# Depthwise convolution of a two-layer encoder: five of eight channel tiles move from VectorE taps to TensorE, and all eight use 32x32 array tiles

## The chip, the cores and the metric

The kernel runs on one core of a Trainium2 chip. The metric is the device time of one execution in microseconds (us). Before the change it is 1244.36 us, the median of three runs (1243.08 to 1247.17). Lower is better.

The core has four compute engines with instruction queues of their own: TensorE (PE in the profile, its weight loads PEld), VectorE (DVE), ScalarE (ACT) and GpSimd (POOL). SyncE (SP) only issues transfers here, and GpSimd issues some too. Matmul results go to PSUM banks, which VectorE and ScalarE read; everything else lies in SBUF, on 128 partitions, or in memory.

## What is computed

One step of a two-layer encoder over 1152 tokens: 1024 of a new stream (the prompt) and 16 of each of 8 running streams (the samples). Layer 0 is attention beside a gated mixing branch. The change lies in layer 1, the convolution layer:

```python
xn = _rmsnorm(x, norm_g)
z = jnp.einsum('btd,de->bte', xn, w_in)              # 1024 -> 3 x 1024
a, b, g = jnp.split(z, [C_WIDTH, 2 * C_WIDTH], axis=-1)
u = a * jax.nn.sigmoid(b)
# 30 earlier rows of u stand ahead: zeros for the prompt, conv_state for each sample
ctx = jnp.concatenate([conv_state, u], axis=1)
c = lax.conv_general_dilated(ctx, w_dw[:, None, :], window_strides=(1,), padding='VALID',
                             feature_group_count=C_WIDTH) + b_dw     # 31 taps per channel
c = jax.nn.silu(_layernorm(c, ln_g, ln_b)) * jax.nn.silu(g)
y = x + jnp.einsum('btc,cd->btd', c, w_out)
return y, ctx[:, -(CONV_WIDTH - 1):]
```

All arithmetic is to the accuracy of float32. A final RMS norm follows.

## The kernel before

**The order.** The program is written in Python; a scheduler places each instruction on its engine's queue by a simulated timeline, so the order on an engine isn't that of the source alone. `issue_after(m)` keeps what is inside it behind the instruction m; `high_priority` moves what is inside forward by an offset. Buffers come from pools with a fixed count (`bufs`); who asks for a buffer waits until its last reader is done.

**Products.** A float32 product is made of three (`mm3`): both operands are split into a high and a low part, and hi·hi, hi·lo and lo·hi are summed in a PSUM bank. A product over 1024 inputs is 24 matmuls ("mm" in the profile). `split_w` fetches weights as raw (SP, three buffers), casts them to wh on ScalarE (L143) and takes wl = raw − wh on VectorE (L144); the pool has four buffers of each. Plain float32 matmuls go through PE in two passes, and the profile has two records for each.

**The convolution layer** (`phase_conv`, `conv_tile`) handles 8 tiles of 128 channels, channels on partitions. For each tile there are three chunks of 384 tokens, and for each chunk two mm3 products of 24: first for b, whose sigmoid ScalarE writes to sb (L1103), then for a, which VectorE multiplies by sb into u. Three PSUM banks hold these products in turn. After each of a tile's six products stands a hook position (0 to 5), at which work of the tile before is put in: at position 1 (`TAIL`) the transposes and copies that write out the last rows of u (un), at the positions in `TOEP` the Toeplitz steps.

Five tiles (0, 1, 3, 5, 7) do the convolution on VectorE (`taps`): 31 instructions over 1024 prompt tokens and 31 over the samples' 8x16. The three tiles of `PE_TILES` (2, 4, 6) do it on TensorE. VectorE writes u to U with time split in 8 phases, U[channel, phase, m]; U is stored to memory (s_u) and read back as X, in which a partition is a pair of channel and phase, 16 channels and 8 phases on 128 partitions, 8 such groups. For a group, five products of 128x128 by 176 columns (py), each with X shifted by one column, make the 31 taps. Their weights tw are block-diagonal, 16 blocks of 8x8, and GpSimd builds them (L1166) from a table wx of shifted taps and the mask `same`. Two groups are a step, at each of four hook positions. ScalarE copies py to Y (L1173); Y goes to memory (s_c, L1176) and comes back as yb with channels on partitions; ScalarE adds the bias into cT (L1180 for the prompt, L1183 twice for the samples). GpSimd sums the cT of tiles 0 to 6 into msum (L952).

Then follow the 8 gate tiles, in pairs that share one load of weights: for each the three mm3 products of the third part of w_in1, and Silu on ScalarE into sg (L1021). After the gate tiles in `LN_AT` stands `norm_chunk`: the layer norm of one 384-token chunk, in which PE sums over channels (ln), ScalarE squares, GpSimd adds squares, and VectorE subtracts the mean and multiplies. At the end VectorE multiplies cT by sg, and the output projection with w_out1 runs over 9 token tiles.

**Setup** (`setup_conv`), long before this layer, transposes the taps and writes tables to memory: s_cc (bias and norm factors, and all taps for VectorE) and s_w (eight shifted copies of the flipped taps of the three tiles).

Of the kernel before, what the change touches and what calls it, by code (L numbers as in the profile page):

```python
# [11 lines left out]
F32 = mybir.dt.float32  # L12
# [10 lines left out]
NB = 8  # L23
# [21 lines left out]
def shape_constants():  # L45
# [26 lines left out]
    same = np.zeros((P, P), np.float32)  # L72
    for p in range(P):
        same[p, p // 8 * 8:p // 8 * 8 + 8] = 1.0
# [7 lines left out]
C_W = C_SAME + P  # L82
PE_TILES = (2, 4, 6)
# [10 lines left out]
TOEP = (2, 3, 4, 5)  # L94
TAIL = 1
LN_AT = (4, 5, 6)
# [6 lines left out]
class Builder:  # L103
# [222 lines left out]
    def setup_conv(self):  # L326
        nc, a = self.nc, self.a
        npe = len(PE_TILES)
        self.s_w = self.dram.tile([npe * P, 8, 40], F32, name="s_w")
        self.s_cc = self.dram.tile([P, 8 * (4 + CONV)], F32, name="s_cc")  # L330
# [9 lines left out]
        nc.gpsimd.dma_start(out=flip, in_=a["cst"][:CONV, C_FLIP:C_FLIP + CONV])  # L340
        ps = self.ptr.tile([P, 512], F32, name="tr")
        for i in range(8):
            nc.tensor.transpose(ps[:, i * CONV:(i + 1) * CONV], wn[:, i * P:(i + 1) * P], self.ident[:CONV, :CONV])
        nc.scalar.copy(cc[:, 32:32 + 8 * CONV], ps[:, :8 * CONV])
        nc.gpsimd.dma_start(out=self.s_cc, in_=cc[:, :32 + 8 * CONV])
        wr = cc[:, 640:640 + npe * 48].rearrange("p (n k) -> p n k", k=48)
        ps = self.ptr.tile([P, 512], F32, name="tr")
        for n, i in enumerate(PE_TILES):
            nc.tensor.matmul(ps[:, n * CONV:(n + 1) * CONV], lhsT=wn[:, i * P:(i + 1) * P], rhs=flip,
                             start=True, stop=True)  # L350
        nc.scalar.copy(wr[:, :, 7:7 + CONV], ps[:, :npe * CONV].rearrange("p (i k) -> p i k", k=CONV))
# [562 lines left out]
    def phase_conv(self):  # L914
        nc, tc, a = self.nc, self.tc, self.a
        with ExitStack() as st:
# [5 lines left out]
            self.pacc = pl.enter_context(tc.tile_pool(name="pac", bufs=1, space=PSUM, reuse_waits="tile"))  # L922
            self.py = self.pacc.tile([P, 512], F32, name="py")
# [5 lines left out]
            cT = [cp.tile([P, TOK], F32, name=f"cT{i}") for i in range(8)]  # L929
            msum = cp.tile([P, TOK], F32, name="msum")  # L930
            cc = cp.tile([P, 8 * (4 + CONV)], F32, name="cc")
            same = cp.tile([P, P], F32, name="same")
            nc.sync.dma_start(out=cc, in_=self.s_cc)
            nc.sync.dma_start(out=same, in_=a["cst"][:, C_SAME:C_SAME + P])
            chan = cc[:, :32].rearrange("p (i n) -> p i n", n=4)
            wdw = cc[:, 32:].rearrange("p (i k) -> p i k", k=CONV)
            npe = len(PE_TILES)
            s_u = self.dram.tile([npe, P * 8, 180], F32, name="s_u")
            s_c = self.dram.tile([npe, P * 8, 176], F32, name="s_c")
            s3 = E(ExitStack())  # L940
            u_p = s3.enter_context(tc.tile_pool(name="up", bufs=2, side="right", reuse_waits="tile"))
            with tc.tile_pool(name="ub", bufs=2, reuse_waits="tile") as ub:
                prev = None
                self.last_tap = None

                def finish(i, f):
                    if f is not None:
                        f()
                    if i == 1:
                        nc.gpsimd.tensor_tensor(msum, cT[0], cT[1], ALU.add)  # L950
                    elif 1 < i < 7:
                        nc.gpsimd.tensor_tensor(msum, msum, cT[i], ALU.add)  # L952

                for i in range(8):
# [3 lines left out]
                    if prev is not None:  # L958
                        hooks[TAIL] = [prev[0]]
                        for p, f in zip(TOEP, prev[1]):  # L960
                            hooks.setdefault(p, []).append(f)
# [100 lines left out]
    def conv_tile(self, i, wb, pm, u_p, ub, cv, chan, wdw, scr, same, hooks):  # L1062
# [100 lines left out]
        def step(q):  # L1163
# [10 lines left out]
            if q < 3:  # L1174
                return
# [37 lines left out]
```

## Time and profile before

| | |
|---|---|
| median of three runs | 1244.36 us (1243.08 to 1247.17) |
| the profiled execution's own time | 1244.07 us |
| its span in the profile | 1242.3 us |
| mean granted TensorE clock | 0.975 of full speed |
| PE busy | 1163.6 us, 94% |
| DVE busy | 807.9 us, 65% |
| ACT busy | 461.0 us, 37% |
| POOL busy | 364.3 us, 29% |

The profile is of one execution. The span runs from the first to the last recorded instruction, and the time of the execution has 1.8 us around it. A row of a group of instructions names the line in the kernel, the engine, the operation, what is written and read (out<-in by the program's names), shapes, the count, the busy time and the mean of one; behind the bar at its end, the engine's idle time ahead of it and who ended it. A wait row reads: engine, waiting tile and line, the releaser, total us, times, longest. The convolution layer and the gate tiles lie between about 776 and 1160 us of the span.

### The profile page before, as it was taken

To read this page: it belongs to the slowest core of one execution; us is meant where nothing else is said; L and a number is where in the kernel's file an instruction comes from. 1 tells how busy PE (TensorE), PEld (TensorE's weight loads), DVE (VectorE), ACT (ScalarE), POOL (GpSimd) and SP (SyncE) were. 2 spreads that over 40 slices of the span, in tenths; PEclk is the share of its full clock that TensorE was granted. 3 is DMA by queue.
4 is the path that set the end of the run, shared out by engine and by line. 5 is a ranking of instruction groups with operands and counts; after the bars stand their busy time and mean duration, and the time that the engine had idled before them with its cause. 6 is when DMAs were issued, how large, how long until landed. Compare 5 with 4: busy or idle time off the path is not lost.

```text
span 1242.3 us, 18215 instructions
## 1 busy us (share of the span) xinstructions
PE 1163.6 (94%) x6516; PEld 1038.4 (84%) x6516; DVE 807.9 (65%) x1663; ACT 461.0 (37%) x1058; POOL 364.3 (29%) x516
## 2 busy tenths in 40 slices
PE   6999999999989997779999998999999987998997
PEld 4878998999989987557776767999999987997886
DVE  5420225688787778765555444899989999267843
ACT  4431223545454545554435334111121212256421
POOL 2232223344354335322322220112424220033300
PEclk9999999999989998889999999999999998999999
DMA  8352444414141314877766646113321310212231
GB/s 298 107 157 73 148 145 136 126 55 120 41 122 46 103 49 137 287 246 238 238 220 237 194 145 174 45 41 89 97 85 60 112 60 24 68 35 102 80 124 68
DMA packets 122042, 153.23 MB, mean 123 GB/s; under 512 B 13697, under 2 KB 85401, under 8 KB 121944
## 3 DMA queue, kind: packets, MB, share of 16 engines
q1 hardware_dynamic: 107968, 108.21, 28.1%
q0 software_dynamic: 13840, 43.60, 10.5%
q8 instruction: 52, 0.85, 0.3%
q14 instruction: 38, 0.31, 0.1%
q10 hardware_dynamic: 144, 0.26, 0.1%
HBM read 116.22 MB, written 36.26 MB: 123 GB/s over the span
## 4 chain that ended last, share of the span: by engine, by line
PE 75%; DMA 9%; DVE 6%; issue 5%; ACT 3%; POOL 1%; SPq 0%; DVEq 0%; POOLq 0%; ACTq 0%
PE mm L155 51%; PE out L155 7%; PE py L1172 3%; PE pa L587 2%; PE tr L416 2%; DMA vraw<-in_cache_v 1%; PE tr L165 1%; PE S L544 1%; PE mm L784 1%; PE S L545 1%; PE mm L783 1%; PE tr L582 1%; DMA big<-s_c 1%; DMA s_c<-big 1%; PE S L730 1%
## 5 line engine op out<-in xcount | busy, mean ns | idle before, releaser
L155 PE MATMUL mm<-yh,wh 128*128 128x384 f32 x576 | 196.4, 341 | 15.2 <-ACT sg L1021 12.7
L155 PE MATMUL mm<-yh,wl 128*128 128x384 f32 x576 | 195.4, 340 | 0.2 <-DVE wl L144 0.2
L155 PE MATMUL mm<-yl,wh 128*128 128x384 f32 x576 | 195.4, 339 | 0.0
L155 PE MATMUL mm<-wh,xh 128*128 128x384 f32 (+1 forms) x504 | 185.4, 369 | 1.5 <-DVE sg L467 0.6
L1148 DVE SCALAR_TENSOR_TENSOR acc<-u,cc,acc 128x1024 f32<-128x1024 f32 x145 | 185.7, 1281 | 0.4
L155 PE MATMUL mm<-wl,xh 128*128 128x384 f32 (+1 forms) x504 | 184.3, 366 | 1.5 <-DVE wl L144 1.5
L155 PE MATMUL mm<-wh,xl 128*128 128x384 f32 (+1 forms) x504 | 183.5, 364 | 0.0
L144 DVE TENSOR_TENSOR wl<-raw,wh 128x1024 fp32r<-128x1024 f32 (+1 forms) x72 | 91.3, 1275 | 91.8 <-ACT wh L143 88.4
L155 PEld LDWEIGHTS mm<-yh,wh 128*128 128x128 f32 x576 | 109.2, 190 | 16.0 <-ACT sg L1021 13.0
L155 PEld LDWEIGHTS mm<-yh,wl 128*128 128x128 f32 x576 | 109.1, 190 | 0.6 <-DVE wl L144 0.5
L155 PEld LDWEIGHTS mm<-yl,wh 128*128 128x128 f32 x576 | 109.2, 190 | 0.3
L155 PEld LDWEIGHTS mm<-wh,xh 128*128 128x128 f32 x504 | 95.7, 190 | 13.1 <-issue 1.1
L155 PEld LDWEIGHTS mm<-wl,xh 128*128 128x128 f32 x504 | 95.6, 190 | 11.4 <-DVE wl L144 2.9
L155 PEld LDWEIGHTS mm<-wh,xl 128*128 128x128 f32 x504 | 95.5, 189 | 8.8 <-DVE xl L168 0.3
L143 ACT CAST wh<-raw 128x1024 fp32r<-128x1024 f32 (+1 forms) x72 | 71.4, 1001 | 70.0 <-PE mm L155 32.2
L124 POOL TENSOR_TENSOR rr<-pw,mhalf 128x1 f32<-128x1 f32 x59 | 38.4, 651 | 165.9 <-DVE pw L123 157.4
L558 ACT ACTIVATE e<-S,nm 128x512 f32<-128x512 f32 (+5 forms) x96 | 55.0, 578 | 53.7 <-DVE nm L553 36.2
L155 PE MATMUL out<-wh,ch 128*128 128x512 f32 x144 | 59.9, 416 | 1.7 <-DVE xr L844 1.2
L1166 POOL TENSOR_TENSOR tw<-wx,same 128x640 f32<-128x640 f32 x24 | 37.3, 1558 | 82.3 <-PE py L1172 72.5
L550 DVE TENSOR_REDUCE nm<-S 128x1 f32<-128x512 f32 (+5 forms) x96 | 52.5, 551 | 10.5 <-PE S L545 9.7
L155 PE MATMUL out<-wh,cl 128*128 128x512 f32 x144 | 58.8, 408 | 0.0
L155 PE MATMUL mm<-wl,ch 128*128 128x512 f32 x144 | 56.4, 392 | 2.3 <-DVE wl L144 2.2
(282 smaller groups left out, 2400.0 us busy)
## 6 DMA issues: line engine op xcount, KB each, us to landing
raw<-in_cache_k SPq DMA_DIRECT2D x32, 512.0 KB, 4.4
vraw<-in_cache_v POOLq DMA_DIRECT2D x32, 512.0 KB, 5.4
raw<-in_w_in SPq DMA_DIRECT2D x24, 512.0 KB, 5.1
raw<-in_w_out SPq DMA_DIRECT2D x16, 512.0 KB, 4.6
raw<-in_w_in SPq DMA_DIRECT2D x32, 256.0 KB, 3.4
raw<-in_w_in SPq DMA_DIRECT2D x48, 128.0 KB, 3.1
s_y<-xr POOLq DMA_DIRECT2D x9, 512.0 KB, 4.7
x<-s_y SPq DMA_DIRECT2D x9, 512.0 KB, 4.2
```

Of the source, the lines that this page charges most:

```text
L124: m = nc.gpsimd.tensor_tensor(out, v[:, :w], self.mhalf[:, :w], ALU.pow)
L143: nc.scalar.copy(h[:, :ks * n], raw[:, :ks * n])
L144: (low or nc.vector).tensor_tensor(l[:, :ks * n], raw[:, :ks * n], h[:, :ks * n].bitcast(F32), ALU.subtract)
L155: m = self.nc.tensor.matmul(out, lhsT=x, rhs=y, start=(i == 0), stop=(i == n - 1))
L165: nc.tensor.transpose(ps[:, k * P:(k + 1) * P], src[:, kk * P:(kk + 1) * P], self.ident)
L416: nc.tensor.transpose(ps[:, h * P:(h + 1) * P], src[:, h * P:(h + 1) * P], self.ident)
L550: nc.vector.tensor_reduce(nm[:, j:j + 1], s[:, :n], AX.X, ALU.max, negate=True)
L558: nc.scalar.activation(e[:, j * n:(j + 1) * n], S[j][:, :n], AF.Exp, bias=nv, accum_out=zz[:, j:j + 1])
L587: nc.tensor.matmul(po, lhsT=wT[:, k * P:(k + 1) * P], rhs=hd["v"][:, k, :], start=(k == 0), stop=(k == qb))
L1148: tap = nc.vector.scalar_tensor_tensor(cv[:, :T] if k == CONV - 1 else acc, u[:, k:k + T], w1, acc, ALU.mult, ALU.add)
L1166: nc.gpsimd.tensor_tensor(tw.rearrange("p s (c f) -> p s c f", f=8), wx[:, g, :].rearrange("p (s f) -> p s f", f=8).unsqueeze(2).broadcast ...
L1172: nc.tensor.matmul(py, lhsT=tw[:, 4 - s, :], rhs=X[:, g, s:s + 176], start=(s == 0), stop=(s == 4))
```

## The change

All eight tiles do the convolution on TensorE; `taps`, the u buffers and the table of taps in s_cc go, and setup makes s_w for eight tiles.

A step is now half a tile: four of the eight groups at once, in two steps at hook positions 3 and 4 of the next tile. X is as before, but a product takes 32 of its 128 partitions (4 channels by 8 phases), with weights of 32x32, and writes 32 partitions of a bank. For each of five shifts s, group j and row position r there is one product, 5·4·4 = 80 a step, from partitions 32r and up to partitions 32c and up of bank py_j, with c = (r + j) mod 4. So for one s the sixteen products stand on the sixteen 32x32 positions of the array, and the four that share a bank come from four row positions. Four PSUM banks hold py. The steps have high priority with an offset of 400. As Y's partitions are rotated, the way to memory (s_c) is seven transfers instead of one.

The bias moves to VectorE (`back`, three instructions a tile). Tile i's bias is added after the first u product of tile i + 2 (`late`); that of tile 6 after gate tile 0, that of tile 7 after gate tile 1. Tile 7's steps stand after the first and second product of gate tile 1 (`hooks_of(8)`). The first two sg buffers move to another pool, and "big" (U, X, Y, yb) has four buffers instead of three. The layer norm's chunks follow gate tiles 3, 4, 5, and the first two quarters of w_out1's first half are fetched and split after gate tile 4, the other two after the gates.

```diff
-    same = np.zeros((P, P), np.float32)
+    same = np.zeros((P, 32), np.float32)
...
-        same[p, p // 8 * 8:p // 8 * 8 + 8] = 1.0
+        same[p, p % 32 // 8 * 8:p % 32 // 8 * 8 + 8] = 1.0
...
-PE_TILES = (2, 4, 6)
...
-TOEP = (2, 3, 4, 5)
+TOEP = (3, 4)
+HPT = 400
...
-LN_AT = (4, 5, 6)
+LN_AT = (3, 4, 5)
...
-            self.py = self.pacc.tile([P, 512], F32, name="py")
+            self.py = [pyp.tile([P, 512], F32, name=f"py{i}") for i in range(4)]
...
+            sg = [cp.tile([P, TOK], F32, name=f"sg{i}") for i in range(2)]
...
+            def back(i):
+                tiles[i][2]()
+                if i == 1:
+                    nc.gpsimd.tensor_tensor(msum, cT[0], cT[1], ALU.add)
+                elif 1 < i < 7:
+                    nc.gpsimd.tensor_tensor(msum, msum, cT[i], ALU.add)
+
+            def hooks_of(i):
+                hooks = {}
+                if i > 0:
+                    hooks[TAIL] = [tiles[i - 1][0]]
+                    for p, f in zip(TOEP, tiles[i - 1][1]):
+                        hooks.setdefault(p, []).append(f)
+                return hooks
+
+            for i in range(8):
+                wb = self.split_w(wp, [a["w_in1"][:, i * P:(i + 1) * P],
+                                       a["w_in1"][:, D + i * P:D + (i + 1) * P]], 256)
+                late = (lambda j=i - 2: back(j)) if i > 1 else None
+                tiles.append(self.conv_tile(i, wb, pm, ub, cT[i], chan, (s_u, s_c), same, hooks_of(i), late))
...
+            def gate_tile(i, wb):
+                i2 = i % 2
+                for c in range(3):
...
+                    nc.scalar.activation(sg[i][:, ts_], ps[:, :384], AF.Silu)
+                    if i < 2:
+                        with tc.issue_after(last):
+                            for f in hooks_of(8).get(3 * i + c, ()):
+                                f()
+                return last
+
+            for i in range(2):
+                if i == 0:
+                    wb = self.split_w(wp, [a["w_in1"][:, 2 * D:2 * D + 256]], 256)
+                gate_tile(i, wb)
+                if i == 0:
+                    back(6)
+            back(7)
...
+            for j in range(1, 4):
+                wb = self.split_w(wp, [a["w_in1"][:, 2 * D + j * 256:2 * D + (j + 1) * 256]], 256)
                 for i2 in range(2):
                     i = 2 * j + i2
...
+                    last = gate_tile(i, wb)
+                    if i == LN_AT[1]:
+                        wo = [self.split_w(wp, [a["w_out1"][:, :512]], 512, p) for p in range(2)]
                     if i in LN_AT:
                         norm_chunk(LN_AT.index(i), last)
-            wb = [self.split_w(wp, [a["w_out1"][:, :512]], 512)]
+            wo += [self.split_w(wp, [a["w_out1"][:, :512]], 512, p) for p in (2, 3)]
+            wb = [sum(wo, [])]
...
-            if pe:
-                dst = U[:, :, 4 + 48 * c:4 + 48 * c + n // 8].rearrange("p f m -> p m f")
-                nc.vector.tensor_tensor(dst, pa_[:, :n].rearrange("p (m f) -> p m f", f=8),
...
+            mu = nc.vector.tensor_tensor(dst, pa_[:, :n].rearrange("p (m f) -> p m f", f=8),
+                                         sb[:, :n].rearrange("p (m f) -> p m f", f=8), ALU.mult)
+            if c == 0 and late is not None:
+                with tc.issue_after(mu.ins if hasattr(mu, "ins") else mu):
+                    late()
...
-            def taps():
...
-                    for k in range(CONV):
...
-                            nc.vector.scalar_tensor_tensor(cvs if k == CONV - 1 else acs, us[:, :, k:k + NQ], w1,
-                                                           acs, ALU.mult, ALU.add)
-                            tap = nc.vector.scalar_tensor_tensor(cv[:, :T] if k == CONV - 1 else acc, u[:, k:k + T], w1,
-                                                                 acc, ALU.mult, ALU.add)
...
-            for g in (2 * q, 2 * q + 1):
-                tw = ub.tile([P, 5, P], F32, name="tw", bufs=3)
...
-                py = self.py[:, g % 2 * 256:g % 2 * 256 + 176]
+            tw = ub.tile([P, 20, 32], F32, name="tw", bufs=2)
...
+            with tc.high_priority(offset=HPT):
                 for s in range(5):
-                    nc.tensor.matmul(py, lhsT=tw[:, 4 - s, :], rhs=X[:, g, s:s + 176], start=(s == 0), stop=(s == 4))
-                nc.scalar.copy(Y[:, g, :], py)
-            if q < 3:
+                    for j in range(4):
+                        for r in range(4):
+                            rs, c = slice(r * 32, (r + 1) * 32), (r + j) % 4
+                            nc.tensor.matmul(self.py[j][c * 32:(c + 1) * 32, q * 256:q * 256 + 176],
+                                             lhsT=tw[rs, j * 5 + 4 - s, :], rhs=X[rs, 4 * q + j, s:s + 176],
+                                             start=(s == 0), stop=(s == 4))
+            for j in range(4):
+                nc.scalar.copy(Y[:, 4 * q + j, :], self.py[j][:, q * 256:q * 256 + 176])
+            if q == 0:
                 return
-            nc.sync.dma_start(out=s_c[n].rearrange("(g p) m -> p g m", p=P), in_=Y)
...
+            for j in range(4):
+                k = j * 32
+                nc.sync.dma_start(out=sv[:P - k, j::4], in_=Y[k:, j::4])
+                if j:
+                    nc.sync.dma_start(out=sv[P - k:, j::4], in_=Y[:k, j::4])
+            yb = ub.tile([P, 8, 176], F32, name="big", bufs=4)
+            nc.sync.dma_start(out=yb, in_=s_c[i].rearrange("(p f) m -> p f m", f=8))
...
-            nc.scalar.activation(cv[:, :T].rearrange("p (m f) -> p m f", f=8),
-                                 yb[:, :, :P].rearrange("p f m -> p m f"), AF.Identity, bias=bia)
...
+        def back():
+            yb, bia = ret["yb"], chan[:, i, 0:1]
+            nc.vector.tensor_scalar(cv[:, :T].rearrange("p (m f) -> p m f", f=8),
+                                    yb[:, :, :P].rearrange("p f m -> p m f"), bia, None, ALU.add)
...
+        return tail, [lambda q=q: step(q) for q in range(2)], back
```

On PE a Toeplitz step stands as a block between mm products, before and after. py is the bank of one step; before, the block of one group, with the mm rows around it:

```order
L155 MATMUL mm<-yl_8095,wh 128x384
L1172 MATMUL py<-big,tw 128x176 x5
L155 MATMUL mm<-yh_8094,wl 128x384
L155 MATMUL mm<-yh_8094,wh 128x384
```

After, the first rows of the block of one step; rows like these, x4 each, go round the four banks five times (20 rows, 80 products):

```order
L156 MATMUL mm<-yh_8089,wl 128x384
L1150 MATMUL py_8242<-big,tw 32x176 x4
L1150 MATMUL py_8243<-big,tw 32x176 x4
L1150 MATMUL py_8244<-big,tw 32x176 x4
L1150 MATMUL py_8245<-big,tw 32x176 x4
L1150 MATMUL py_8242<-big,tw 32x176 x4
```

The eight blocks of five a tile become two blocks of 80.

On VectorE, around the end of tile 7 and the first gate tile (cT_8257, 8258 and 8259 are tiles 5, 6 and 7; "big" written by L1108 is tile 7's U; L145 splits weights):

```order
L1169 TENSOR_SCALAR cT_8257<-big,cc 128x1024
L1172 TENSOR_SCALAR cT_8257<-big,cc 128x8x8 x2
L1108 TENSOR_TENSOR big<-mm,sb 128x48x8
L145 TENSOR_TENSOR wl<-raw,wh 128x1024
L1169 TENSOR_SCALAR cT_8258<-big,cc 128x1024
L1172 TENSOR_SCALAR cT_8258<-big,cc 128x8x8 x2
L1108 TENSOR_TENSOR big<-mm,sb 128x32x8
L1114 TENSOR_TENSOR utmp_8250<-mm,sb 128x160
L145 TENSOR_TENSOR wl<-raw,wh 128x1024 x2
L1169 TENSOR_SCALAR cT_8259<-big,cc 128x1024
```

The bias of tile 6, written after gate tile 0 in the source, has been placed ahead of the last u product of tile 7.

On ScalarE, where the gate begins; before (cT_8260 is tile 6):

```order
L1173 COPY big<-py 128x176 x2
L1180 ACTIVATE cT_8260<-big,cc 128x1024
L1183 ACTIVATE cT_8260<-big,cc 128x8x8 x2
L1021 ACT_TABLE_LOAD
L1021 ACTIVATE sg_10366<-mm 128x384 x3
L1021 ACTIVATE sg_10367<-mm 128x384 x2
```

and after:

```order
L144 CAST wh<-raw 128x1024 x2
L968 ACT_TABLE_LOAD
L968 ACTIVATE sg_8260<-mm 128x384 x2
L1124 COPY un<-trb 128x128
L1125 COPY un<-trb 30x128
L968 ACTIVATE sg_8260<-mm 128x384
L968 ACTIVATE sg_8261<-mm 128x384
L1154 COPY big<-py_8242 128x176
```

No bias stands ahead of the gate's activations any more.

169 lines of the change are left out of this document (52 added, 117 removed).

## The prediction

> **What bounds the kernel now.** I began with the page's busy shares, then cut the convolution layer into stretches, then asked for TensorE's waits there. Times are us from the span's start.
>
> ```profile
> PE 1163.6 (94%) x6516; PEld 1038.4 (84%) x6516; DVE 807.9 (65%) x1663; ACT 461.0 (37%) x1058; POOL 364.3 (29%) x516
> ...
> 776.00:840.00 64.00, 64.00 (x375) 63.75 (x374) 55.66 (x76) 10.97 (x21) 9.11 (x11) 1.00 0.15 42
> 905.00:970.00 65.00, 62.56 (x365) 62.11 (x365) 62.69 (x84) 11.20 (x24) 21.46 (x19) 0.97 0.27 82
> 970.00:1033.00 63.00, 50.06 (x300) 49.35 (x298) 61.60 (x83) 13.25 (x26) 17.54 (x14) 0.92 0.26 83
> 1033.00:1085.00 52.00, 51.69 (x289) 51.69 (x290) 30.02 (x40) 10.44 (x18) 1.23 (x1) 0.96 0.13 41
> 1128.00:1159.00 31.00, 27.37 (x120) 20.99 (x119) 29.08 (x61) 21.10 (x54) 10.44 (x7) 1.00 0.23 85
> ```
> After the stretch and its length, a row gives the busy time of PE, PEld, DVE, ACT, POOL and the granted clock. In the convolution loop PE and VectorE are both nearly full; PE has holes only in 905:1033 and 1128:1159. So VectorE's fullness costs time only where PE waits for it. PE's waits from 776 to 1160 (us in total, times, longest):
>
> ```profile
> PE mm L155 <- ACT sg L1021: 12.7, 1, 12.7
> PE py L1172 <- DMA big<-s_u: 3.0, 2, 2.4
> PE mm L155 <- ACT sb L1103: 2.5, 1, 2.5
> PE mm L155 <- DVE wl L144: 2.2, 1, 2.2
> PE mm L155 <- DVE x L1053: 0.8, 1, 0.8
> PE mm L155 <- ACT ch L1046: 0.5, 1, 0.5
> ```
> TensorE sets the end, with one large hole. ScalarE's rows with two of the chain of waits say whose it is:
>
> ```profile
> 1020.64 0.30 ACT L1173 COPY big<-py 128x176 f32<-128x176 f32 x1 [1.91 <-PE py L1172]
> 1028.84 2.03 ACT L1180 ACTIVATE cT<-big,cc 128x1024 f32<-128x1024 f32 x1 [7.90 <-DMA big<-s_c]
> 1032.77 1.25 ACT L1021 ACTIVATE sg<-mm 128x384 f32<-128x384 f32 x3
> ...
> 1020.97 3.71 DMA s_c<-big
> 1024.75 4.07 DMA big<-s_c
> ```
> Tile 6's result goes out to memory and back; its bias activation waits on ScalarE for it, and three gate activations, which alone release PE's banks, stand behind.
>
> **The change part by part.**
>
> *The taps.* Five tiles of 31 wide and 31 narrow taps leave VectorE.
>
> ```profile
> L1148 DVE SCALAR_TENSOR_TENSOR acc<-u,cc,acc 128x1024 f32<-128x1024 f32 x145 | 185.7, 1281 | 0.4
> L1172 PE MATMUL py<-big,tw 128*128 128x176 f32 x240 | 40.1, 314 | 3.0 <-DMA big<-s_u 3.0
> ```
> The first row alone is 185.7 us. On the path I count them as nothing: the waits above name no tap. Their value is that Toeplitz work may replace them.
>
> *The Toeplitz products.* One block before, one mm stretch of 96, and a long stretch after the hole (from the chain):
>
> ```profile
> 853.40 1.49 PE py L1172 x10
> 797.45 16.67 PE mm L155 x96
> 1033.32 51.73 PE mm L155 x288
> ```
> Five products are ten records (two passes each) in 1.49. Before: 24 blocks, 35.8 us. After: 16 steps, each 80 products on 32x32 tiles. If all sixteen tiles run together a step is again five rounds of two passes, 1.49; if nothing but the four column positions overlap it is four times that, 5.96. The trace has no 32x32 product, but score products on four 32-column positions:
>
> ```profile
> 512.25 1.50 PE L730 MATMUL S<-KT,qz 128*32 128x256 f32 x24
> 513.57 0.64 PE L730 MATMUL S<-KTx,qz 128*32 128x272 f32 x8
> ...
> 563.90 0.40 PE L786 MATMUL mm<-vs,wt 128*128 128x512 f32 x1
> 564.23 0.64 PE L730 MATMUL S<-KT,qz 128*32 128x256 f32 x8
> 564.80 1.09 PE L416 MATMUL tr<-cst,raw 128*128 128x128 f32 x8
> ```
> 24 records begin within 513.57 − 512.25 = 1.32, six groups of 0.22; one 256-column pass alone would be 0.149 × 256/176 = 0.217. So four column positions overlap with no loss. I take the near end for rows too, since that row also streams four separate operands through the same partitions. Going into and out of that mode costs: 0.33 from the 512-column product to the group instead of about 0.22, and 0.57 for two passes of 0.217, so 0.11 + 0.14. With as much again for sixteen staggered starts and sixteen loads I put a step at 1.9: 16 × 1.9 = 30.4, **−5.4**. Ends: 23.8 (−12.0) and 95.4 (+59.6).
>
> The Trainium skill, "TensorE: Matmul & The Clock Gate", Part 3, reports 16 tiles of K=M=32 at 10.6 times one tile's rate; by that an estimate is 1.49 × 16/10.6 = 2.25 a step, 36.0 in all, and the sum below would be 5.6 us longer. No run here shows a 32x32 product.
>
> *Bias off ScalarE, two tiles later.* The activations L1180 and L1183 become VectorE instructions, so nothing stands before the gate's activations: **−12.7**. The 288 products after the hole took 51.73 against 288 × 16.67/96 = 50.0, at a clock of 0.96 where 776:840 has 1.00; with the hole that goes: **−1.7**. The 2.5 behind sb is the activation table at the start and stays.
>
> *The round trips.* X waits are 3.0 in 905:1033. A step now comes 96 products after its tile's last one instead of 72 or less, so these go: **−3.0**. Rows for what follows:
>
> ```profile
> L1173 ACT COPY big<-py x24: 305/306/308, 854.9 to 1020.6; 128x176 f32<-128x176 f32 x24
> L1109 DVE TENSOR_TENSOR big<-mm,sb x9: 651/917/945, 822.8 to 975.4; 128x384 f32<-128x384 f32 x6, 128x256 f32<-128x256 f32 x3
> L1117 POOL COPY big<-utmp x3: 439/1361/1368, 841.8 to 976.3; 128x128 f32<-128x128 f32 x3
> L1180 ACT ACTIVATE cT<-big,cc x3: 2032/2192/2193, 900.1 to 1028.8; 128x1024 f32<-128x1024 f32 x3
> L1176 SPq DMA_DIRECT2D s_c<-big x3: 366/367/367, 892.2 to 1021.0; - x3
> ...
> raw<-in_w_in SPq DMA_DIRECT2D x48, 128.0 KB, 3.1
> s_u<-big SPq DMA_DIRECT2D x3, 720.0 KB, 3.8
> big<-s_u SPq DMA_DIRECT2D x3, 720.0 KB, 4.6
> ...
> L952 POOL TENSOR_TENSOR msum<-msum,cT 128x1152 f32<-128x1152 f32 x5 | 13.3, 2664 | 31.8 <-ACT cT L1183 28.2 <-DVE cT L1148 3.6
> ```
> Let T be the end of a tile's second step. Four copies of 0.31 and seven issues of 0.37 end near T + 2.6; a piece of this size lands 3.1 later, T + 5.7; the read back takes 4.07, T + 9.8. In tiles 2 to 7 the bias follows the next tile's first product, 24 + 48 products later (T + 12.5): no wait. That next tile's s_u stands behind this read on SP's queue: issued near T + 6.2, X there at T + 6.2 + 3.8 + 4.6 = T + 14.6; its step is due at T + 20.9. Hidden; six us of cover.
>
> *Where the wait goes.* On VectorE the bias of tile 6 stands before tile 7's last product (order rows above). It holds VectorE until T + 9.8, runs some 2.5 (ScalarE's 2.1 for the wide part, two narrow ones), then 0.65 + 0.3 for the product and utmp: T + 13.2. Queued behind it: PE's third group from there needs that bank at 4.17 × 3 = T + 12.5, the state transposes stand there too: 0.7. GpSimd then adds cT of tile 6 to msum (2.66) before it copies utmp (0.44): U is whole at T + 15.4, not T + 6, and X at T + 15.4 + 3.8 + 4.6 = T + 23.8 against T + 20.9 + 0.7: 2.2 more. **+2.9**; with quicker landings 0, with slower ones 7. The bias of tile 7 blocks only weights due 25 us later: nothing.
>
> *LN one gate tile sooner, W_out halves early.* The three last waits (3.5) fall in 1128:1159, where VectorE is busy 29 of 31 us; LN's third chunk gets two gate tiles of cover, not one: **−3.5**. But W_out's first two parts now take weight buffers between gate pairs 2 and 3, so pair 3's casts wait for gate tile 5's last products: a cast and a subtraction (about 1.0 and 1.23) against 2.1 us of products left, twice, with LN work ahead on both engines: **+1.5** (0 to 6). The setup's wider tables, the strided products and the larger pools have idle engines around them: nothing.
>
> Sum: −5.4 − 12.7 − 1.7 − 3.0 + 2.9 − 3.5 + 1.5 = −21.9. The profiled execution took 1244.07 (span 1242.3, 1.8 around it), 0.3 under the median, so 1222.2 there and **1222.5** beside the median.
>
> **The rivals.**
>
> *Round trips late everywhere.* The six us of cover is the sum of four landings in seven pieces; if they come 8 us later, PE waits 2 us in each of seven tiles: +14, 1236. For it: PE waited for big<-s_u twice already. Against: DMA was at 0.27 in 905:970.
>
> *Weights four at a time.*
>
> ```profile
> L730 PEld LDWEIGHTS S<-KT,qz x192: 106/109/177, 512.3 to 682.1; 128*32 128x32 f32 x192
> ```
> Four 32-column loads of 0.108 are in flight together; a pass now has sixteen. If they go by fours, a pass is 0.43, a step 4.3: (4.3 − 1.9) × 16 = +38, 1261. For it: nothing shows more than four. Against: the row above hid four loads behind every pass. It decides from 3.3 a step on, where the sum is zero.
>
> *Rows take turns (the other side).* The four products of one bank py_j come from four row positions. If such products run one after the other, a step is 5.96: +65, 1288, slower. Against it: they write different partitions, and the column rows show no loss for sharing one bank. The Trainium skill, "TensorEngine Tiling (Array Packing)", Restrictions and Gotchas, Gotcha 1, says that different row tiles cannot access the same PSUM bank at once; read to the letter it is this rival. Its worst form is issue: the score row's 24 records begin 1.32/24 = 0.055 apart, and at that 160 records take 8.8 a step: 1333.
>
> **How the numbers follow.** Forecast, sixteen together: 0.60, 1222, own range 1212 to 1232. Late round trips, or steps of 2.5 to 3: 0.13, 1232 to 1241. Weights by fours: 0.13, around 1261. Rows in turn or issue-bound: 0.14. The range 1212 to 1262 leaves out the last and half of the weights' case. 0.3% (3.7 us) is about what can be told from no change. Faster: 0.60 + 0.11; same: 0.06, from the edges of the second and third case; slower: 0.23.
>
> **What would show it.** Right: step blocks near 1.9 on PE, no wait for sg after the last step, one wait of 2 to 3 us for big<-s_u before tile 7's first step, DVE under 70% in the loop. Wrong: the 80 products over 3.3 us, PE waiting for s_u in every tile, or a gap at gate tile 6 above 6 us.

## The result, and the profile after

The changed kernel takes 1256.7 us (median of four runs, 1254.4 to 1258.2) against 1245.8 for the kernel before: 1.0089 times as long, 95% interval 1.0068 to 1.0111. In a second series it was 1257.1 against 1246.1 (1.0087, 1.0070 to 1.0104). Forecast were 1222.5 and a gain of 22; it is a loss of 11.

The busy shares of the profile after, whose own run took 1256.6 us:

```profile
PE 1178.2 (94%) x8838; PEld 1036.8 (83%) x8838; DVE 593.8 (47%) x1377; ACT 461.2 (37%) x1088; POOL 357.0 (28%) x518
```

VectorE has lost 214 us of work (807.9 before) and TensorE has gained 15. TensorE's waits between 776 and 1175 us of the profile after (total, times, longest):

```profile
PE py L1150 <- DMA big<-s_u: 5.5, 1, 5.5
PE ln L1011 <- POOL ac L1007: 2.8, 2, 1.5
PE mm L156 <- ACT sb L1103: 2.5, 1, 2.5
PE mm L156 <- ACT sg L968: 1.2, 1, 1.2
PE mm L156 <- DVE wl L145: 1.1, 2, 0.7
PE ln L1012 <- POOL ac L1007: 0.9, 2, 0.6
```

The 12.7 behind sg is gone, as forecast, and so are the 3.0 for X in the tile loop. New are 5.5 for X of tile 7 and 3.7 for ac of the layer norm. Waits alone do not make a loss, though. A Toeplitz step after the change, in TensorE's timeline (start, us); 1.9 was forecast, and the block of one group before took 1.49 by the prediction's row:

```profile
844.44 2.72 PE L1150 MATMUL py<-big,tw 32*32 32x176 f32 x160
```

The table cuts each profile at the starts of five products on PE: the first of the convolution layer, of gate tile 0, of gate tile 6, of the output projection, and then the span's end. All numbers in us; the rows under the changed kernel's three are experiments that follow below.

| profile | layer starts at | tile loop | gate tiles 0-5 | gate tiles 6, 7 | output | layer in all |
|---|---|---|---|---|---|---|
| before | 755.7 | 244.5 | 99.8 | 30.9 | 111.3 | 486.5 |
| changed | 762.3 | 252.8 | 92.9 | 38.8 | 107.9 | 492.4 |
| changed, second | 758.5 | 253.4 | 93.5 | 37.3 | 109.1 | 493.3 |
| changed, third | 757.9 | 253.4 | 93.4 | 37.3 | 109.2 | 493.3 |
| back6 | 759.9 | 252.0 | 86.8 | 37.3 | 109.8 | 485.9 |
| ln_before | 764.1 | 253.4 | 91.7 | 30.9 | 111.3 | 487.2 |
| ln_before, second | 757.1 | 252.4 | 90.6 | 30.9 | 111.3 | 485.2 |
| both_back | 761.5 | 250.3 | 84.4 | 30.9 | 111.3 | 476.9 |
| bl_gate_only | 757.9 | 249.2 | 87.8 | 30.9 | 111.4 | 479.2 |
| mix_4_4 | 753.7 | 245.6 | 77.8 | 30.9 | 111.9 | 466.2 |
| mix_4_4, second | 756.1 | 247.3 | 77.8 | 30.9 | 111.5 | 467.5 |

In the layer the change gains 6 to 7 in gate tiles 0 to 5 and 2 to 3 in the output, and loses 8 to 9 in the tile loop and 6 to 8 in gate tiles 6 and 7: 6 to 7 lost in all. In the first profile another 6.6 lay ahead of the layer. The kernel before has one profile only, and its tile loop was a quick one: bl_gate_only, and s4_setup_after below, whose loops have the same work, took 249.2 and 249.0 there, so that the loss in the loop is 4 to 9.

### The profile page after: what moved, and what is told of

It is laid out like the page before. It is cut to its first block, busy times and chain, and to the rows that moved or that the text cites. A ratio compares the mean times of both kernels' runs of the same rounds, so it can differ in the third digit from the quotient of the medians.

```text
span 1254.8 us, 22769 instructions
## 1 busy us (share of the span) xinstructions
PE 1178.2 (94%) x8838; PEld 1036.8 (83%) x8838; DVE 593.8 (47%) x1377; ACT 461.2 (37%) x1088; POOL 357.0 (28%) x518
## 5 line engine op out<-in xcount | busy, mean ns | idle before, releaser
L145 DVE TENSOR_TENSOR wl<-raw,wh 128x1024 fp32r<-128x1024 f32 (+1 forms) x72 | 88.6, 1238 | 205.5 <-ACT wh L144 199.3
L156 PEld LDWEIGHTS mm<-wl,xh 128*128 128x128 f32 x504 | 96.0, 190 | 10.5 <-DVE wl L145 1.8
L125 POOL TENSOR_TENSOR rr<-pw,mhalf 128x1 f32<-128x1 f32 x59 | 33.7, 571 | 182.3 <-DVE pw L124 173.4
L1108 DVE TENSOR_TENSOR big<-mm,sb 128x384 f32<-128x384 f32 (+1 forms) x24 | 20.1, 837 | 96.5 <-PE mm L156 69.5
L156 PE MATMUL out<-wl,ch 128*128 128x512 f32 x144 | 58.2, 404 | 0.0
L156 PE MATMUL mm<-wh,ch 128*128 128x512 f32 x144 | 56.6, 393 | 0.5 <-ACT ch L1055 0.5
```

The source lines that it names most:

```text
L125: m = nc.gpsimd.tensor_tensor(out, v[:, :w], self.mhalf[:, :w], ALU.pow)
L145: (low or nc.vector).tensor_tensor(l[:, :ks * n], raw[:, :ks * n], h[:, :ks * n].bitcast(F32), ALU.subtract)
L156: m = self.nc.tensor.matmul(out, lhsT=x, rhs=y, start=(i == 0), stop=(i == n - 1))
L1108: mu = nc.vector.tensor_tensor(dst, pa_[:, :n].rearrange("p (m f) -> p m f", f=8), sb[:, :n].rearrange("p (m f) -> p m f", f=8), ALU.mult)
```

## The experiments

Unless said otherwise an experiment edits the changed kernel.

**Is layer 0 late because its order changed?** The larger setup makes the scheduler place layer 0's instructions in another order on every engine. Two kernels cross this: the changed kernel with the setup of before (s3), in which layer 0 has the order of before, and the kernel before with the setup of the change (s4).

```diff
-        self.s_w = self.dram.tile([8 * P, 8, 40], F32, name="s_w")
+        self.s_w = self.dram.tile([npe * P, 8, 40], F32, name="s_w")     # s3: all of setup_conv as before
...
-        nc.sync.dma_start(out=wx, in_=self.s_w[i * P:(i + 1) * P]...
+        nc.sync.dma_start(out=wx, in_=self.s_w[i % 3 * P:(i % 3 + 1) * P]...
```

> The changed kernel with the setup of before: tables for three tiles only, which all eight tiles use in turn (so the convolution's numbers are wrong, its work is not changed). With it every engine's order up to the convolution layer is that of before. Theory, order: the changed setup moved the order of layer 0 and that costs the 6.6 us by which the layer's first product starts later (762.3 against 755.7); here it starts at 755.7 +- 1 and the time is 1250, 6 to 7 under the changed kernel. Rival, data: the five more tables and their transfers, or the run itself, make layer 0 late; then with the order restored it starts at 760 or later and the time stays within 2 of 1256.7.

> The kernel before with the setup of the change: tables for all eight tiles, of which three are used, and none for the taps on VectorE, which read other numbers (their output is wrong, their work is not changed). Every engine's order up to the convolution layer is that of the changed kernel. Theory, order: the first product of the layer starts at 762.3 +- 1 and the time is 1252, 6 to 7 over before. Rival, convolution layer: what is late in the changed kernel comes from its own later work, so this one starts at 755.7 and takes 1245 to 1247.

Measured: s3 1247.5 (1.0007, 0.9984 to 1.0030), the layer's start at 759.3; s4 1249.9 (1.0034, 1.0011 to 1.0057), the start at 756.7. By the start both miss: with the order of before the layer did not start sooner than with that of the change. s3 is faster than the changed kernel for another reason: its scheduler put the bias of tile 6 behind tile 7's u, as back6 below does on purpose, and back6, with the changed layer 0, takes 1246.2. The two differ in layer 0's order and agree within 1.4. So by the starts and by this pair the order is not the cause; only s4, 4.4 over the kernel before, speaks for it. Why s4 is slower stays open; its profile has more waiting for X (4.4 against 3.0) and a granted clock of 0.98 in the loop against 0.99. Over the nineteen profiles of this study the start lies between 752.6 and 764.1, and two profiles of one kernel, on two chips, differ by 7 (764.1 and 757.1). That this is scatter between executions and not the chip is likely but not shown: on three chips the kernel before has medians within 0.7 (1245.4, 1246.1, 1246.0), and on each of them its times range over 9 to 12.

**The bias of tile 6 on VectorE.**

```diff
-                nc.vector.tensor_tensor(utmp, pa_[:, 224:384], sb[:, 224:], ALU.mult)
+                ut = nc.vector.tensor_tensor(utmp, pa_[:, 224:384], sb[:, 224:], ALU.mult)
+                self.last_u = ut.ins if hasattr(ut, "ins") else ut
...
                 if i == 0:
-                    back(6)
+                    with tc.issue_after(self.last_u):
+                        back(6)
```

> The changed kernel with the bias of tile 6 held on VectorE behind the last product of tile 7; nothing else in the order changes. Theory, VectorE blocked: the bias waits for its round trip and holds tile 7's u, so X comes late; the one wait of 5.5 for big<-s_u and the 0.6 beside it go, U is whole some 10 us sooner, and the time falls by 5 to 6.5, to 1251. Rival, slow landing: s_u takes 6.2 us to land here whatever the order, and the wait keeps 2 us or more; the fall is under 4. Rival, covered: what is gained is lost at the layer norm's last chunk, which is paced by its own chain; no change over 2 us.

Measured: 1246.2 (1.0014, 0.9994 to 1.0033), 10.5 to 10.9 under the changed kernel; the layer takes 485.9, 6.5 to 7.4 less (expected for the time: 5 to 6.5), nearly all of it in gate tiles 0 to 5. VectorE's timeline of the changed kernel, with the idle time ahead in brackets:

```profile
1014.13 1.23 DVE L145 TENSOR_TENSOR wl<-raw,wh 128x1024 fp32r<-128x1024 f32 x1 [11.90 <-ACT wh L144]
1021.70 1.21 DVE L1169 TENSOR_SCALAR cT<-big,cc 128x1024 f32<-128x1024 f32 x1 [6.34 <-DMA big<-s_c]
1022.83 0.44 DVE L1172 TENSOR_SCALAR cT<-big,cc 128x64 f32<-128x64 f32 x2
1023.20 0.64 DVE L1108 TENSOR_TENSOR big<-mm,sb 128x256 f32<-128x256 f32 x1
1023.67 0.32 DVE L1114 TENSOR_TENSOR utmp<-mm,sb 128x160 f32<-128x160 f32 x1
```

and the same place in back6:

```profile
1010.85 1.23 DVE L145 TENSOR_TENSOR wl<-raw,wh 128x1024 fp32r<-128x1024 f32 x1 [11.90 <-ACT wh L144]
1012.02 0.67 DVE L1109 TENSOR_TENSOR big<-mm,sb 128x256 f32<-128x256 f32 x1
1012.53 0.32 DVE L1115 TENSOR_TENSOR utmp<-mm,sb 128x160 f32<-128x160 f32 x1
1019.07 1.21 DVE L1171 TENSOR_SCALAR cT<-big,cc 128x1024 f32<-128x1024 f32 x1 [6.22 <-DMA big<-s_c]
```

Tile 7's u followed the split of weights at once; in the changed kernel it stood 7.8 behind a bias that waited for its round trip. What came after it there, on GpSimd and on SP's queue:

```profile
1023.42 2.66 POOL L944 TENSOR_TENSOR msum<-msum,cT 128x1152 f32<-128x1152 f32 x1 [10.75 <-DVE cT L1172]
1026.02 1.43 POOL L1115 COPY big<-utmp 128x128 f32<-128x128 f32 x1
```

```profile
1027.60 0.47 SPq L1133 DMA_DIRECT2D s_u<-big  x1
1033.81 0.37 SPq L1135 DMA_DIRECT2D big<-s_u  x1
```

The sum of cT delays the copy, the copy takes 1.43, and the store lands after 6.2. In back6 the wait for X is 1.3 instead of 5.5. The first reading holds. The landing is slow there too (the read is issued 8.2 after the store), but the store starts 9 us sooner after tile 6's step, so the rival's wait of 2 us or more is not there. The wait of 5.5 costs more than its length: without it, the step behind it still takes 4.2 to 4.5 between its neighbours' starts in the three profiles of the changed kernel, where the median step takes 2.9. That the median falls by some 3 us more than the profiled layer, to 1246 and not 1251, is not explained.

**The layer norm one tile sooner and the early quarters of w_out1.**

```diff
-LN_AT = (3, 4, 5)
+LN_AT = (4, 5, 6)
...
-                    if i == LN_AT[1]:
-                        wo = [self.split_w(wp, [a["w_out1"][:, :512]], 512, p) for p in range(2)]
...
-            wo += [self.split_w(wp, [a["w_out1"][:, :512]], 512, p) for p in (2, 3)]
-            wb = [sum(wo, [])]
+            wb = [self.split_w(wp, [a["w_out1"][:, :512]], 512)]
```

> The changed kernel itself once more, on the chip of the next two. Theory, scatter: layer 0, whose first product of the convolution layer has started anywhere from 752.6 to 762.3 in eight profiles, whatever the order, owes some 4 of the 6.6 us to that one execution; then the time here is 1250 to 1253, and the profile shows the wait of about 5 for big<-s_u again. Rival, constant: 1256 to 1258 as in the first four runs, with the layer's start after 760.

> The changed kernel with the layer norm's chunks behind gate tiles 4, 5, 6 and the whole first half of w_out1 after the gates, as before the change. Theory, own chain: a norm chunk follows the one before it at 22 to 27 us, so an earlier start gains nothing at the end, while the waits for gate tile 6's weights (2.3 in the profile) and those in PE's queue for ac (2.0) go; the time is 2 to 4 under after_again. Rival, cover: one gate tile less of cover makes the last chunk later by some us; the time is 2 or more over after_again.

Measured: the changed kernel again 1257.1, the rival's value, though its profiled run, at 1253.7 its fastest, started the layer at 758.5. ln_before takes 1244.7 (0.9986, 0.9971 to 1.0001): 12.3 less, three times the 4 that was the most expected. Its layer is 5 to 8 shorter over the two profiles. The two parts of the edit were not run apart; what belongs to which is read from the traces. Gate tiles 6 and 7 in the timeline of the changed kernel:

```profile
1110.21 0.44 PE L156 MATMUL mm<-yh,wh 128*128 128x384 f32 x1 [1.19 <-ACT sg L968]
1111.57 0.44 PE L156 MATMUL mm<-yh,wl 128*128 128x384 f32 x1 [0.74 <-DVE wl L145]
...
1117.44 0.38 PE L1011 MATMUL ln<-ones,ac 128*128 128x1 f32 x2 [1.27 <-POOL ac L1007]
...
1118.39 0.38 PE L1012 MATMUL ln<-ones,ac 128*128 128x1 f32 x2 [0.28 <-POOL ac L1007]
...
1120.28 0.53 PE L156 MATMUL mm<-yh,wh 128*128 128x384 f32 x1
```

The first two waits are for the pair's weights (wh was late too: that wait is put down to an activation between), two are for ac, and behind these stand products of 0.53 instead of 0.33. The granted clock (0.89, ahead of the DMA share) in a stretch of it, in the first profile:

```profile
1115.00:1130.00 15.00, 13.45 (x66) 12.08 (x65) 3.65 (x10) 4.23 (x10) 4.21 (x5) 0.89 0.09 31
```

The lower clock has no fixed place: over gate tiles 6 and 7 it is 0.96 in the first profile but 0.99 and 1.00 in the other two, which have 0.95 over the output stage instead. More products of the layer norm stand in gate tiles 6 and 7, too. GpSimd adds the squares of one chunk in 9.5 to 9.8 us, and PE's queue now reaches the sums before these are done:

```profile
1108.56 9.78 POOL L1007 TENSOR_TENSOR ac<-ac,sq 128x384 f32<-128x384 f32 x6 [13.91 <-ACT sq L1003]
...
1135.37 9.73 POOL L1007 TENSOR_TENSOR ac<-ac,sq 128x384 f32<-128x384 f32 x6 [14.56 <-ACT sq L1003]
```

Here is the same row in the second profile of ln_before, in which the output projection starts at 1131.0:

```profile
1143.74 9.59 POOL L1007 TENSOR_TENSOR ac<-ac,sq 128x384 f32<-128x384 f32 x6 [17.81 <-ACT sq L1003]
```

There the third chunk runs under the output projection, whose first six token tiles don't need it. It had cover enough with the old place.

**Both edits together**, with further profiles for the scatter:

> back6 and ln_before together. Theory, two separate losses: from the layer's first product to the end it takes 478 to 481, and the time is 12 or more under after_again's 1257.1 by the profiles (6.5 + 5.7) and up to 23 by the medians; 1236 to 1241. Rival, one loss seen twice: either edit only shifts the same late work, so both together stay at 1244 to 1246.

> The changed kernel, third profile. Theory, layer itself: the layer's first product at 755 to 760 and 494 to 498 from there to the end. Rival, layer 0: 760 to 764 and 492 to 493.

> ln_before, second profile. Its first one, at 1253.2, had the layer's first product at 764.1 and 487.2 behind it. Theory, layer 0 scatters: a run of 1242 to 1247 has its first product at 754 to 758 and again 486 to 488 behind it. Rival: the start stays at 760 or later and the layer takes 482 to 484.

Measured: both_back 1240.3 (0.9945, 0.9921 to 0.9970), 16.8 under the changed kernel; its layer takes 476.9, 16.4 less. The losses are separate and, in the layer, add up (7.1 and 6.8 alone, 16.1 together, by the means of the profiles); by the medians they do not quite (10.9 and 12.3 alone, 16.8 together). The third profile of the changed kernel is of a run of 1253.0 with the start at 757.9 and 493.3 behind it: between the two theories. The second profile of ln_before has the start that the theory gave, and a layer just under it: 1244.2, start 757.1, layer 485.2.

**The gate hole alone.** Before, with tile 6's bias still on ScalarE but behind the gate's first activations:

```diff
+            ret["yb"] = yb
+            if i != 6:
+                back()
...
+                last, act = gate_tile(i, wg)
+                if i == 0:
+                    with tc.issue_after(act):
+                        finish(6, back6)
```

> The kernel before with one part of the change alone: tile 6's bias stays on ScalarE but stands behind the gate's first activations (its yb lies in a buffer of u, and the gate's buffers are taken from the pool's other end). Theory, the hole is order alone: the 12.7 us wait for sg goes and the 1 to 2 us of slower clock behind it; the time is 1231 to 1233, 13 to 14 under before, with the three Toeplitz tiles and the taps as they were. Rival, the hole moves: the layer norm at the end, which needs tile 6 and tile 7, becomes late by what the gate gains; gain under 7.

Measured: 1233.3 (0.9894, 0.9858 to 0.9930), 12.2 less than before, and gate tiles 0 to 5 go from 99.8 to 87.8. ScalarE's timeline there:

```profile
1027.49 0.31 ACT L1190 COPY big<-py 128x176 f32<-128x176 f32 x1 [1.91 <-PE py L1189]
1027.82 1.28 ACT L982 ACT_TABLE_LOAD   x1
1029.11 1.26 ACT L982 ACTIVATE sg<-mm 128x384 f32<-128x384 f32 x3
```

Only the load of the activation table stands between tile 6's last copy and the gate, and of the wait of 12.7 for sg 2.2 are left. The hole was order, and the rest of the change was not needed to close it.

**What a Toeplitz step costs.** Six small edits of the products; where a product leaves out part of a bank, VectorE also clears the banks once. In all six the scheduler also placed tile 6's bias behind tile 7's u, wholly or its last part, so they are compared by their steps and not by their times. (That its place changed by itself in edits that don't concern it shows how near a tie it was.)

```diff
-    lhsT=tw[rs, j * 5 + 4 - s, :], rhs=X[rs, 4 * q + j, s:s + 176], ...
+    rhs=X[rs, 4 * q + j, s:s + 88]                  # step_n88; out 88 columns
+    rhs=X[rs, 4 * q + j // 2 * 2:4 * q + j // 2 * 2 + 2, s:s + 176]   # step_n352
+    lhsT=tw[rs, j * 5 + 4 - s, :16]                 # step_w16; out 16 partitions
+    self.py[r][...] instead of self.py[j][...]      # step_bank
+    for r in range(2)                               # step_two_rows
+    for r outside, for j inside                     # step_rows_outer
```

> The changed kernel with half the columns in every Toeplitz product (88 of 176; the other half of the convolution is left out, and the banks are cleared once by VectorE). In the changed kernel a step takes 2.72 us: after a first burst its 160 passes (a weight load and a matmul each) begin 16.7 ns apart. Theory, rate of instructions: PE takes a pair every 16.7 ns whatever it streams, so the step stays at 2.6 to 2.75. Rival, streams: sixteen tiles overlap only in part and the columns set the pace; then the step falls to 1.4 to 1.6.

> The changed kernel with twice the columns in every Toeplitz product (352; the result is another one). Theory, rate of instructions: 16 pairs need 0.267 us, and 352 columns at the 0.149 per 176 of the step before need 0.298, so the step becomes 3.0 to 3.2 for twice the work. Rival, streams: 5.2 to 5.5.

> The changed kernel with weights of 16 columns instead of 32 in every Toeplitz product (half the outputs are left out). Theory, rate of instructions: 2.6 to 2.75 as before. Rival, weight loads: the 16.7 ns are the 32 columns of a load, one load at a time; then a pair takes about half and the step falls to 1.5 to 1.9.

> The changed kernel with the bank chosen by the row position instead of the group, so that no two row positions share a bank (the result lies in other places and comes out wrong). Theory, rate of instructions: nothing changes, 2.6 to 2.75. Rival, shared bank: the products of four row positions hinder each other in one bank; without that the step falls to the forecast's 1.5 to 1.9.

Steps in the timelines of step_n88, step_n352 and step_bank:

```profile
834.43 1.99 PE L1152 MATMUL py<-big,tw 32*32 32x88 f32 x160
```

```profile
847.27 4.19 PE L1152 MATMUL py<-big,tw 32*32 32x352 f32 x160
```

```profile
842.28 2.72 PE L1150 MATMUL py<-big,tw 32*32 32x176 f32 x160
```

For the columns neither theory holds. From the product before a step to the one behind it, less one product, the three widths take 2.02, 2.75 and 4.22: 0.73 more for 88 columns, 1.47 more for the next 176, which is 1.29 + 0.00833 a column. Ten passes of 0.833 ns a column are full overlap of all sixteen positions (before: 0.149 us for 176, 0.847 ns a column). On top lie 1.29 a step, 0.129 a pass, that the columns don't hide. step_w16 took 2.68, so half the weights' columns take off only 0.07, and its rival falls. But the loads themselves are little shorter there (0.086 to 0.093 us, against 0.101 to 0.104 with 32 columns), so this run doesn't say that loads cost nothing. step_bank took 2.75: sharing a bank costs nothing here, and the rival of row positions that take turns falls.

> The changed kernel with the row positions 0 and 1 alone: 40 products a step on eight array tiles (half the convolution is left out, the banks are cleared once). Theory, a fixed time of a pass: the next pass on an array tile starts 0.13 us after the stream of the last one ends, however many tiles there are; the step stays at 2.6 to 2.75. Rival, time of a pair: 8 ns for each load with its matmul, so half of 1.29 goes and the step takes 2.05 to 2.2.

> The changed kernel with the sixteen products of a shift issued row position by row position (four columns positions each) instead of group by group; the result is the same. Theory, a fixed time of a pass or of a pair: 2.7 to 2.8 again. Rival, order: loads hide behind streams of other rows only if these are in flight already; then the step changes by 0.3 or more, up or down.

A step in the timeline of step_two_rows:

```profile
838.24 1.72 PE L1152 MATMUL py<-big,tw 32*32 32x176 f32 x80
```

Eight positions take 1.75 between the neighbours, under both expectations: 1.49 + 0.26, nearly the forecast's form. Sixteen take 1.00 more for the same ten passes, 0.10 a pass. step_rows_outer took 2.75; the order of the sixteen is no matter. A 32x32 load takes 0.101 to 0.104 in the trace (median 0.104), so what sixteen positions add is as much as one load a pass that is no longer hidden. That it is this load, and why eight hide it, no run here shows.

**A version with both.** bl_gate_only with 32x32 steps for tiles 0, 2, 4, 6 and taps for 1, 3, 5, 7:

```diff
-PE_TILES = (2, 4, 6)
+PE_TILES = (0, 2, 4, 6)
...
-                    acc = self.pacc.tile([P, T], F32, name="acc")
-                    acs = self.pacc.tile([P, NB, NQ], F32, name="acs")
+                    acc, acs = cv[:, :T], cvs        # sums in SBUF; the banks hold py
...   # step() as in the change
```

> bl_gate_only with four tiles (0, 2, 4, 6) as Toeplitz products on 32x32 positions, four py banks, and four (1, 3, 5, 7) as taps on VectorE, whose sums stand in cT instead of PSUM; biases on ScalarE two tiles later. From the trace, PE pays 8 steps of 2.86 = 22.9 instead of 24 blocks of 1.50 = 35.9, and VectorE has one tile of taps less. Theory, TensorE bound: 13 under the 1233.3 of bl_gate_only, 1218 to 1224. Rival, VectorE bound: taps in SBUF or in the way of the u products hold PE's banks, and the gain is under 5.

> mix_4_4, second profile; the first, at 1221.8, was the fastest of its runs (median 1227.8), with the first product at 753.7. Theory, layer 0 scatters: a run of 1226 to 1232 starts the layer at 757 to 763 and takes 466 to 468 from there. Rival: the start is the same and the layer takes 470 or more.

Measured: 1227.8 (0.9858, 0.9828 to 0.9888), 18.3 under the kernel before and 29 under the changed one. By the medians it is 5.5 under bl_gate_only, not 13; the layer is 12 to 13 shorter in the profiles, but bl_gate_only's profiled run was its slowest and both of mix_4_4 lie under its median. By the table, gate tiles 0 to 5 fall by 10 (five blocks, 7.5, and the last 2.2 behind sg are gone), and the tile loop by 2 to 4, where 19 blocks (28.4) gave way to 8 steps (22.9). The second profile's waits:

```profile
PE py L1203 <- DMA big<-s_u: 7.4, 2, 4.3
PE mm L156 <- DVE wl L145: 2.3, 2, 2.2
PE py L1203 <- issue: 2.0, 2, 1.1
PE mm L156 <- DVE big L1138: 1.2, 1, 1.2
```

Here X is late twice, and only one wait of 1.2 is for VectorE's u. In the first profile it is the other way: 2.5 for X, but 2.7 for VectorE's u and 1.4 for its utmp. So both engines hold PE up in turn, and the medians give neither theory's number. The second profile fits the scatter of layer 0 only in part: 1225.5, start at 756.1, layer 467.5. It is the fastest kernel of this study.

## Why the prediction was wrong

By its own steps, in the layer; the sum forecast was −21.9, the profiles show +6 to +7, the medians +11.

| step | forecast | shown | by |
|---|---|---|---|
| Toeplitz products | −5.4 | +9.8 | 16 x 2.86 = 45.7 against 24 x 1.50 = 35.9, with the slower neighbours |
| gate hole, and clock behind it | −12.7, −1.7 | −12.0 | bl_gate_only, gate tiles 0-5: 99.8 to 87.8 |
| X in the tile loop | −3.0 | −2.7 | waits: 3.0 before, 0.3 (issue) after |
| bias of tile 6 in VectorE's queue | +2.9 | +6.5 to +7.4 | back6 |
| layer norm sooner, w_out1 early | −3.5, +1.5 | +5 to +8 | ln_before, twice |

The shown column adds to 6.6 to 10.5. In bl_gate_only 2.2 of the gate hole are left that the changed kernel doesn't have; with these off the sum is 4.4 to 8.3, about the layer's 6 to 7.

**The step that failed first is the form of a Toeplitz step.** Taking 1.49 for ten passes was right, for eight positions and for sixteen, and "four column positions overlap with no loss" did carry over to rows. What was wrong is the term of 0.41 for entering, leaving, starts and loads: it was scaled from four positions, and at sixteen it is 1.26, and 0.11 more in the products beside it. So 16 x 0.96 = 15.4 of the 28 by which the layer missed its forecast lay in one term that no row showed. The rival "weights four at a time" (4.3 a step) put the loss in the loads, which no run here shows or rules out, and at a size too large; "steps of 2.5 to 3" stood in the chances with 1232 to 1241 and was what came, but not alone. The rival of rows in turn fell, and with it the reading to the letter of the Trainium skill, "TensorEngine Tiling (Array Packing)", Restrictions and Gotchas, Gotcha 1: two layouts of the banks took the same 2.75. The Trainium skill's "TensorE: Matmul & The Clock Gate", Part 3, gave 10.6 times one tile's rate, by which 2.25 a step was estimated; measured is 1.49 x 16 / 2.75 = 8.7, so its estimate was the nearer one and still short.

**The wait on VectorE was named rightly and mis-sized.** Every link was there: bias, u, sum on GpSimd, copy, store, read. Tile 7's u was ready 13.1 after tile 6's step, 13.2 forecast: the seven issues took longer and the bias less. Then the copy was counted at 0.44, the least of its row, whose median is 1.36, and took 1.43; and s_u landed after 6.2, not the 3.8 of three transfers before. These 3.4 make 5.6 of 2.2, and the wait was 5.5; the layer lost 6.5 to 7.4 by it, because the step behind the wait was slower, too.

**The layer norm's step had the wrong cause.** The 3.5 in 1128:1159 were waits for weights (2.2), x (0.8) and ch (0.5), not for the norm: with the norm a tile sooner the 0.5 for ch is still there. The output stage did get 2 to 3 shorter, and the wait for weights in it fell to 0.3, which speaks for the early quarters of w_out1. By the traces, starting the norm sooner gained nothing, because its third chunk had run under the output projection, and cost 3.7 of waits for ac in PE's queue; products behind such waits took 0.53 instead of 0.33. The prediction priced the weights' wait there (1.5 against 2.3 with its neighbours) and left out that PE would reach ac too early.

**"The setup has idle engines around it: nothing"** overlooked that it changes layer 0's order. s3 and back6 differ in it and agree within 1.4; s4's 4.4 is the one sign that it may matter.

**What stays open:** some 4 of the 11 us. The layer's profiles show 6 to 7; the profiled runs of the changed kernel (1253.0, 1253.7, 1256.6) lie under its median and that of the kernel before (1244.1) under its own, the start of the layer varies by more than the rest, and the tile loop of before varies for the same work (244.5 to 249.2), so profiles don't settle it. Equally open is why sixteen positions cost 0.10 a pass that eight don't.

## What to carry to other kernels

A mode that no row shows should be priced with its fixed cost per pass as an unknown of its own: here the streams overlapped as hoped, and the fixed part, three times what was forecast, was the largest single part of the miss. An in-order engine with slack is no free place for an instruction that waits for a round trip: name what stands behind it, and put it after that work. And before a change is taken whole, its parts are worth running alone: of this one the order of three activations was worth 12 us, and the rest together cost 23 (1233.3 to 1256.7).

## What the runs showed of the hardware

Sixteen 32x32 float32 products overlap fully in their streams (0.833 ns a column and pass at 88, 176 and 352 columns), with 0.129 us a pass on top; with eight the same ten passes of 176 columns take 1.75 instead of 2.75. Four row positions that write different partitions of one bank take as long as on four banks (2.75). The weights' width hardly counts: 16 columns instead of 32 took 0.07 off a step, and the load itself fell only from 0.104 to 0.088. And one and the same kernel started its second layer 7 us apart in two executions, which were on two chips (757.1 and 764.1), so a stage's gain is better read from that stage than from the end of one profile.
